# A Strassen-type up projection in the MLP of a one-core encoder layer

## Chip, cores and metric

One Trainium2 chip, one of its cores. The metric is the device time of one execution in microseconds. The engines in the profile are PE (TensorE, matmuls), PEld (TensorE's weight loads), DVE (VectorE), ACT (ScalarE), POOL (GpSimd) and SP (SyncE, which issues most DMAs).

## The reference

2176 tokens (2048 of a prompt, 128 of eight running streams) of width 1024 pass one layer:

```
h = rmsnorm(x, ln_mix); z = h @ w_in                       # 1024 x 1280
a = chunk-causal attention(q, k, v of z); b = pooling mixer(u of z)
x = x + concat(rmsnorm(a), rmsnorm(b)) @ w_out             # 1024 x 1024
x = x + square(relu(rmsnorm(x, ln_ffn) @ w_up)) @ w_down   # 1024 x 4096, 4096 x 1024
x = x + sigmoid(rmsnorm(x, ln_ple) @ w_ple_gate) * (p @ w_ple_proj)
y = rmsnorm(x, ln_final)
```

## The kernel before

Activations lie transposed: 128 features on the partitions, tokens along the free axis. The tokens form six blocks, `BLOCKS` = 256, 384, 384, 384, 384, 384. Matrix products are made in three matmuls (`mm3`, lines 117 to 119): each operand is split into a rounded high part and a low part, and high x high, low x high and high x low are summed in PSUM. The split of a weight is in `load_w`: a DMA of 512 KB, a ScalarE cast (L107) and a subtraction (L110) that falls to VectorE and GpSimd in turn, for the gates to GpSimd alone. `split` (L125, L126) and `gain_split` (L190, L191) do the same for activations. `SumSq` (L143, L144) sums squares for a norm; `rstd` and `rstd_dve` make the reciprocal root of it.

The first part, ordered by the string `SEQ_A`, is norm, input projection, attention, pooling and output projection, block by block; `out_proj` writes the new residual to the DRAM tiles `x1d`. The second part takes the blocks in pairs, `SUPER` = (1,2), (3,4), (5,0); a pair is called a super-block here. `mlp_start` loads the two blocks from `x1d` and normalises them (`load_norm`). `mlp` walks over 16 chunks of `FCH` = 2 feature tiles of 128. Per feature tile and block, up is 8 input tiles x 3 = 24 matmuls into one PSUM bank, then the squared ReLU with its split (L662, L666 to L668). Down takes, per block and output tile d, 2 x 3 matmuls and adds the bank to `acc` in SBUF (L682). After the last chunk the third norm is prepared, `gate` runs the gate and the side projection (30 matmuls per output tile), and `finish` writes out. PSUM is used as a ring of seven banks. The order of instructions on each engine is set when the program is built, by a list scheduler; on the chip each engine keeps its order and waits on semaphores.

Of the kernel before, what the change touches and what calls it, by code (L numbers as in the profile page):

```python
# [16 lines left out]
P = 128  # L17
# [9 lines left out]
SEQ_A = "I0 P1 M0 A0 K0 S0 I1 P2 M1 K1 I2 R0 A1 O0 P3 R1 M2 K2 I3 A2 O1 R2 M3 P4 K3 O2 A3 P5 R3 I4 M4 O3 A4 K4 I5 R4 M5 K5 A5 O4 R5"  # L27
SEQ_B = "X1 O5 X2"
# [4 lines left out]
QLENG = lambda nc: nc.vector  # L33
NPR = [128] + BLOCKS[1:]
# [9 lines left out]
FCH = 2  # L44
# [12 lines left out]
def hymba_step(ctx: ExitStack, tc: tile.TileContext, ins, outs):  # L57
# [10 lines left out]
    xhl = ctx.enter_context(tc.tile_pool(name="xhl", bufs=3))  # L68
# [8 lines left out]
    mask = const.tile([P, 256], F32, name="mask")  # L77
    ident = const.tile([P, P], F32, name="ident")
    invc = const.tile([P, NG, 16], F32, name="invc")
# [4 lines left out]

    x1d = [dram.tile([P, KT, n], F32, name=f"x1d{b}") for b, n in enumerate(BLOCKS)]
# [6 lines left out]
    RING = ("mm", "sc", "tr", "mm", "sc", "tr", "pv")  # L92
    ring = [0]

    def ps_ring(nm):
        ring[0] += 1
        return ps_tile(RING[ring[0] % len(RING)], nm)

    cnt = [0]

    def load_w(src, ktiles, width=P, raw_bufs=2, hl_bufs=3, tag="w", pool=None, eng=None):
        pool = pool or wp
        raw = pool.tile([P, ktiles, width], F32, tag=tag + "r", name="wraw", bufs=raw_bufs)
        nc.sync.dma_start(out=raw, in_=src)
        hi = pool.tile([P, ktiles, width], F32R, tag=tag + "h", name="whi", bufs=hl_bufs)
        lo = pool.tile([P, ktiles, width], F32R, tag=tag + "l", name="wlo", bufs=hl_bufs)
        nc.scalar.copy(out=hi, in_=raw)  # L107
        cnt[0] += 1
        eng = eng or (nc.vector if cnt[0] % 2 else nc.gpsimd)
        eng.tensor_tensor(out=lo, in0=raw, in1=hi.bitcast(F32), op=ALU.subtract)  # L110
        return hi, lo

    def mm3(ps, whl, xs, first=True, last=True):
        n = len(xs)
        hi, lo = whl
        for i, (wsel, (xh, xl)) in enumerate(xs):
            nc.tensor.matmul(ps, lhsT=wsel(hi), rhs=xh, start=first and i == 0, stop=False)  # L117
            nc.tensor.matmul(ps, lhsT=wsel(lo), rhs=xh, start=False, stop=False)  # L118
            nc.tensor.matmul(ps, lhsT=wsel(hi), rhs=xl, start=False, stop=last and i == n - 1)  # L119

    def ks(xt, N, kk):
        return [((lambda t, k=k: t[:, k, :]), (xt[0][:, k, :N], xt[1][:, k, :N])) for k in kk]
# [73 lines left out]
    def load_norm(b, src, g, hl, rstd):  # L196
        N = BLOCKS[b]
        sq = SumSq(N)
        for k in range(KT):
            x = row_tile("x")[:, :N]  # L200
            nc.sync.dma_start(out=x, in_=src[:, k, :])
            gain_split(x, g + k, hl[0][:, k, :N], hl[1][:, k, :N], LOENG[k % len(LOENG)](nc))
# [3 lines left out]
    def hl_tile(nm, pool=xhl):  # L206
        h = pool.tile([P, KT, NMAX], F32R, tag="xh", name=nm + "h")
        l = pool.tile([P, KT, NMAX], F32R, tag="xl", name=nm + "l")
        return h, l
# [9 lines left out]
    def out_proj(b):  # L219
# [4 lines left out]
        rb, ra = st_b["rb"], st_b["ra"]  # L224
        for d in range(KT):
# [13 lines left out]
            nc.sync.dma_start(out=x1d[b][:, d, :], in_=xr)  # L239

    xs, rs1 = {}, {}

    def mlp_start(b, rstd):
        xs[b] = hl_tile("x1")
        rs1[b] = load_norm(b, x1d[b], C_GFFN, xs[b], rstd)

    with tc.tile_pool(name="pa", bufs=2) as pa:
        pgain = pa.tile([P, NG], F32, name="pgain", bufs=1)
# [26 lines left out]
        def pool_mix(b, L):  # L275
            st_b = state[b]
            mh, ml = st_b["mx"]
            for g, w in enumerate(POOL_W):
# [13 lines left out]
                mhk, mlk = mh[:, 4 + g, :L], ml[:, 4 + g, :L]  # L292
# [19 lines left out]
        def pool_mix4(b, src, S, L, col):  # L312
# [33 lines left out]
            for g in range(NG):  # L346
                mm3(ps[:, g, :], (wpool_h, wpool_l), [((lambda t, g=g: t[:, g, :]), (dh[:, g, :], dl[:, g, :]))])
# [536 lines left out]
```

## Time and profile before

| | |
|---|---|
| median of 3 runs (2560.92 to 2566.02) | 2564.93 us |
| span of the profiled execution | 2563.4 us |
| PE / PEld busy | 2438.7 / 2361.4 us |
| DVE / ACT / POOL busy | 1814.0 / 874.2 / 827.8 us |
| HBM read and written | 228.44 and 18.36 MB |

The profiled execution's span, from its first instruction to its last, lies 1.5 us under the median and within the three runs. Matmuls are pipelined: the duration of one (about 0.33 us at 384 columns) overlaps the next, so the busy time of PE says that it was occupied, and the distance between starts says how fast it went.

### The profile page before, as it was taken

The page shows a single profiled execution, that of the slowest core. Times are in us where ns is not written, and L with a number is a line of the kernel's source. Part 1 is how long each engine was busy: PE and PEld are TensorE (multiplying, and loading weights), DVE is VectorE, ACT ScalarE, POOL GpSimd, SP SyncE. Part 2 cuts the span into 40 slices and gives each one's busy share as a digit, 9 for nine tenths or more (in the row PEclk, how much of TensorE's full clock was granted, in tenths as well). Part 3 has the DMA queues.
Part 4 walks back from the last instruction along what each step waited for, and adds up shares of the span by engine and source line. Part 5 has one row for each costly group of instructions (what it writes and reads, how often), then busy time and mean ns, then how long its engine had stood idle before and what let it go on. Part 6 is the DMA issues. An engine that isn't in the chain of part 4 may idle for free.

```text
span 2563.4 us, 36604 instructions
## 1 busy us (share of the span) xinstructions
PE 2438.7 (95%) x14324; PEld 2361.4 (92%) x14324; DVE 1814.0 (71%) x3113; ACT 874.2 (34%) x1601; POOL 827.8 (32%) x548
## 2 busy tenths in 40 slices
PE   7889998999899999999998999999999899999986
PEld 7888888998799999999888999999988899999986
DVE  6769888888765555555889555555587966666687
ACT  5446655445421111111652111111165212221254
POOL 4634557454631111111381111111138211111134
PEclk8989999999999999999999999999999999999998
DMA  5424335433732222222244222221234422222223
GB/s 157 129 87 137 95 120 165 138 106 97 249 102 65 59 66 66 63 62 66 91 151 158 66 66 59 66 63 59 61 102 135 136 75 75 83 74 67 83 76 113
DMA packets 104892, 249.17 MB, mean 97 GB/s; under 512 B 19600, under 2 KB 55440, under 8 KB 104720
## 3 DMA queue, kind: packets, MB, share of 16 engines
q1 hardware_dynamic: 104176, 246.32, 31.4%
q8 instruction: 112, 1.84, 0.3%
q10 hardware_dynamic: 544, 0.52, 0.1%
q14 instruction: 60, 0.49, 0.1%
HBM read 228.44 MB, written 18.36 MB: 96 GB/s over the span
## 4 chain that ended last, share of the span: by engine, by line
PE 59%; DVE 10%; ACT 2%; DMA 2%; issue 1%; POOL 0%; SPq 0%; DVEq 0%; ACTq 0%; POOLq 0%
PE ps_dn L117 10%; PE ps_dn L118 10%; PE ps_dn L119 10%; PE ps_up L119 9%; PE ps_up L118 9%; PE ps_up L117 9%; DVE sqa L144 2%; DVE acc L714 1%; DVE x1l L191 1%; DVE x2l L191 1%; DMA x<-x1d 1%; DVE rs_t L159 1%; DMA xr<-in_xT 1%; ACT whi L107 1%; DVE acc L737 1%
## 5 line engine op out<-in xcount | busy, mean ns | idle before, releaser
L110 POOL TENSOR_TENSOR wlo<-wraw,whi 128x1024 fp32r<-128x1024 f32 (+1 forms) x245 | 533.0, 2182 | 1466.9 <-ACT whi L107 1452.1
L107 ACT CAST whi<-wraw 128x1024 fp32r<-128x1024 f32 (+1 forms) x395 | 377.1, 968 | 999.8 <-issue 578.5
L682 DVE TENSOR_TENSOR acc<-ps_dn,acc 128x384 f32<-128x384 f32 (+1 forms) x768 | 389.6, 530 | 167.9 <-PE ps_dn L119 166.9
L117 PE MATMUL ps_dn<-hh,whi 128*128 128x384 f32 (+1 forms) x1536 | 500.0, 327 | 4.5 <-DVE r L662 4.5
L119 PE MATMUL ps_up<-x1l,whi 128*128 128x384 f32 (+1 forms) x1536 | 501.0, 326 | 1.2 <-DVE x1l L191 1.2
L117 PE MATMUL ps_up<-x1h,whi 128*128 128x384 f32 (+1 forms) x1536 | 501.4, 327 | 0.7 <-ACT x1h L190 0.7
L118 PE MATMUL ps_up<-x1h,wlo 128*128 128x384 f32 (+1 forms) x1536 | 501.9, 327 | 0.0
L118 PE MATMUL ps_dn<-hh,wlo 128*128 128x384 f32 (+1 forms) x1536 | 499.4, 327 | 0.0
L119 PE MATMUL ps_dn<-hl,whi 128*128 128x384 f32 (+1 forms) x1536 | 488.0, 326 | 0.0
L117 PEld LDWEIGHTS ps_dn<-hh,whi 128*128 128x128 f32 x1536 | 290.8, 189 | 5.1 <-DVE r L662 5.1
L119 PEld LDWEIGHTS ps_up<-x1l,whi 128*128 128x128 f32 x1536 | 290.2, 189 | 2.0 <-DVE x1l L191 1.5
L117 PEld LDWEIGHTS ps_up<-x1h,whi 128*128 128x128 f32 x1536 | 290.1, 189 | 1.3 <-ACT x1h L190 1.0
L118 PEld LDWEIGHTS ps_up<-x1h,wlo 128*128 128x128 f32 x1536 | 290.3, 189 | 0.7 <-issue 0.6
L118 PEld LDWEIGHTS ps_dn<-hh,wlo 128*128 128x128 f32 x1536 | 290.8, 189 | 0.0
L119 PEld LDWEIGHTS ps_dn<-hl,whi 128*128 128x128 f32 x1536 | 289.0, 189 | 0.2 <-DVE hl L668 0.2
L662 DVE SCALAR_TENSOR_TENSOR r<-ps_up,sqa 128x384 f32<-128x384 f32 x192 | 102.1, 535 | 254.2 <-PE ps_up L119 254.0
L667 DVE TENSOR_TENSOR r<-r 128x384 f32<-128x384 f32 x192 | 191.2, 998 | 97.4 <-ACT hh L666 97.4
L110 DVE TENSOR_TENSOR wlo<-wraw,whi 128x1024 fp32r<-128x1024 f32 x150 | 191.0, 1273 | 56.4 <-ACT whi L107 54.1
L666 ACT ACTIVATE hh<-r 128x384 fp32r<-128x384 f32 x192 | 96.3, 504 | 300.2 <-DVE r L662 300.0
L117 PE MATMUL ps_in<-xnh,whi 128*128 128x384 f32 (+1 forms) x472 | 162.9, 345 | 12.9 <-DVE z L561 5.5
L118 PE MATMUL ps_in<-xnh,wlo 128*128 128x384 f32 (+1 forms) x472 | 161.2, 342 | 2.7 <-POOL wlo L110 2.0
L119 PE MATMUL ps_in<-xnl,whi 128*128 128x384 f32 (+1 forms) x472 | 159.6, 339 | 0.0
(208 smaller groups left out, 3992.4 us busy)
## 6 DMA issues: line engine op xcount, KB each, us to landing
wraw<-in_w_up SPq DMA_DIRECT2D x96, 512.0 KB, 3.7
wraw<-in_w_down SPq DMA_DIRECT2D x96, 512.0 KB, 3.6
wraw<-in_w_in SPq DMA_DIRECT2D x59, 512.0 KB, 3.7
wraw<-in_w_out SPq DMA_DIRECT2D x48, 512.0 KB, 3.7
wraw<-in_w_gate SPq DMA_DIRECT2D x48, 512.0 KB, 3.6
x<-in_xT SPq DMA_DIRECT2D x40, 192.0 KB, 2.6
xr<-in_xT SPq DMA_DIRECT2D x40, 192.0 KB, 3.2
x1d<-xr SPq DMA_DIRECT2D x40, 192.0 KB, 2.1
```

The source lines that it names most:

```text
L107: nc.scalar.copy(out=hi, in_=raw)
L110: eng.tensor_tensor(out=lo, in0=raw, in1=hi.bitcast(F32), op=ALU.subtract)
L117: nc.tensor.matmul(ps, lhsT=wsel(hi), rhs=xh, start=first and i == 0, stop=False)
L118: nc.tensor.matmul(ps, lhsT=wsel(lo), rhs=xh, start=False, stop=False)
L119: nc.tensor.matmul(ps, lhsT=wsel(hi), rhs=xl, start=False, stop=last and i == n - 1)
L144: eng.tensor_tensor(out=o, in0=o, in1=t, op=ALU.add)
L159: V.tensor_tensor(out=u, in0=u, in1=y, op=ALU.mult)
L191: eng.scalar_tensor_tensor(out=lo, in0=src, scalar=c, in1=hi.bitcast(F32), op0=ALU.mult, op1=ALU.subtract)
L662: nc.vector.scalar_tensor_tensor(out=r, in0=ps, scalar=0.0, in1=rs1[b], op0=ALU.max, op1=ALU.mult)
L666: nc.scalar.activation(out=hh, in_=r, func=AF.Square)
L667: nc.vector.tensor_tensor(out=r, in0=r, in1=r, op=ALU.mult)
L682: nc.vector.tensor_tensor(out=acc[b][:, d, :N], in0=ps, in1=acc[b][:, d, :N], op=ALU.add)
```

## The change

Up is done on 2x2 blocks: two feature tiles (output halves), two halves of 512 inputs (4 input tiles each), two halves of the tokens of a super-block. Seven products replace eight, in Strassen's manner with shared sums. With A the weight blocks and B the normalised activations:

```
S1 = A21+A22   S2 = S1-A11   S3 = A11-A21   S4 = A12-S2
T1 = B12-B11   T2 = B22-T1   T3 = B22-B12   T4 = B21-T2
products: A11*B11, S2*T2, A12*B21, S1*T1, S3*T3, S4*B22, A22*T4
```

The weight sums are made on GpSimd in every pass over a feature pair; sums and blocks are then split into high and low parts. The activation operands (7 with high and low part, 4 input tiles each) are made once per super-block, in `comb`, from rows of `x1d` and the roots stored in `rsd`, with four subtractions on GpSimd per step; the four steps are put between output tiles of the block-5 output projection, or of the last down chunk of the super-block before (`fill`). The block products are added on VectorE into rows in SBUF, and the squared ReLU reads SBUF.

The tokens of the second part are cut into six halves of 364, 364, 364, 364, 360, 360 (`CUTS`), so that the two halves of a super-block are equal. Down goes in chunks of `FCH` = 4 feature tiles: 12 matmuls per output tile, half and chunk, 8 chunks; its weight tensor is laid out anew, and a piece of 4 tiles (256 KB) serves both halves, but is loaded for each half in the last chunk. All weights come in such units of 4 tiles, with 6 raw buffers and 5 each for high and low parts. Sums of squares for the MLP norm move from `load_norm` into `out_proj`, the root into `out_fin`, called at the places `F0` to `F4` of `SEQ_A`. The order in the second part: two or three feature pairs of up lead, then each down chunk is followed by two more; the second gate of a super-block (`tail`) stands between feature pairs of the next one. The PSUM ring is divided: up uses the four banks `sc` and `tr`, down and gates the three of `mm` and `pv`.

```diff
-SUPER = [(1, 2), (3, 4), (5, 0)]
+CUTS = [256, 620, 984, 1348, 1712, 2072, 2432]
-FCH = 2
+FCH = 4
+NWR, NWL, NWH = 6, 5, 5
+    def load_u(src, eng=None):
+        raw = wp.tile([P, 4, P], F32, tag="wr", name="wraw", bufs=NWR)
         nc.sync.dma_start(out=raw, in_=src)
         cnt[0] += 1
+        return split_u(raw, eng or (nc.vector if cnt[0] % 2 else nc.gpsimd))
...
     def out_proj(b, fill=()):
+        sq = st_b["sq1"] = SumSq(N)
...
+            sq.add(xr, eng=nc.gpsimd)
+            if d % 2 and fill:
+                fill.pop(0)()
+    def out_fin(b):
+        rs = state[b]["sq1"].rstd(D, ps_tile("ms", "ps_ms"))
+        nc.sync.dma_start(out=rsd[b], in_=rs)
...
+        def comb(s, rs, k):
+            for kk in range(2):
+                for i in range(2):
+                    x = r[kk, i] = row("xr", "xc", n)
+                    for b, c, o in pieces(2 * s + i):
+                        nc.sync.dma_start(out=x[:, o], in_=x1d[b][:, kt, c])
+                    nc.vector.scalar_tensor_tensor(out=x, in0=x, scalar=gain, in1=rs[i], op0=ALU.mult, op1=ALU.mult)
+            put("B11", b11)
+            sub(b11, b12, b11)
+            put("T1", b11)
...
+        def up(s, p):
+            for nm, f, k0 in (("A11", 2 * p, 0), ("A21", 2 * p + 1, 0), ("A22", 2 * p + 1, 4), ("A12", 2 * p, 4)):
+                raw[nm] = raw_u(nm)
+                nc.sync.dma_start(out=raw[nm], in_=w_up[f][:, k0 : k0 + 4, :])
+            wsum("S1", "A21", "A22", ALU.add)
+            wsum("S2", "S1", "A11", ALU.subtract)
+            wt = {"A11": split_u(raw["A11"], nc.vector), "S2": split_u(raw["S2"], nc.vector)}
+            wsum("S3", "A11", "A21", ALU.subtract)
+            wsum("S4", "A12", "S2", ALU.subtract)
+            for nm, eng in zip(WOPS[2:], (nc.gpsimd, nc.vector, nc.vector, nc.vector, nc.gpsimd)):
+                wt[nm] = split_u(raw[nm], eng)
+            def prod(w, o):
+                ps = ps_tile(("sc", "tr")[up_ring[0] % 2], "ps_up")[:, :n]
+                mm3(ps, WU([wt[w]]), [(k, (xh[:, k, :n], xl[:, k, :n])) for k in range(4)])
+            def hidden(x, i):
+                nc.vector.scalar_tensor_tensor(out=x, in0=x, scalar=0.0, in1=x, op0=ALU.max, op1=ALU.mult)
+                split(x, hh[:, i, :n], hl[:, i, :n], nc.vector)
+            nc.scalar.copy(out=x11, in_=prod("A11", "B11"))
+            add(u, prod("S2", "T2"), x11)
+            add(x11, prod("A12", "B21"), x11)
+            hidden(x11, 0)
+            add(v, prod("S1", "T1"), u)
+            p7 = prod("S3", "T3")
+            add(u, p7, u)
+            add(x22, p7, v)
+            hidden(x22, 3)
+            add(v, prod("S4", "B22"), v)
+            hidden(v, 1)
+            add(u, prod("A22", "T4"), u)
+            hidden(u, 2)
...
+        for s in range(3):
+            if s == 0:
+                up(s, 0)
+                up(s, 1)
+            else:
+                up(s, 0)
+                finish(2 * s - 2)
+                tail(s - 1, 2 * s - 1)
+                up(s, 1)
+                finish(2 * s - 1)
+            up(s, 2)
+            acc_load(s)
+            for c in range(NPAIR // 2 - 1):
+                down(s, c)
+                up(s, 2 * c + 3)
+                if 2 * c + 4 < NPAIR:
+                    up(s, 2 * c + 4)
+            fill = [] if last else comb_steps(s + 1)
+            down_last(s, fill)
+            for f in fill:
+                f()
+            tail(s, 2 * s)
```

## Rows read from the trace of the kernel before

**Rows 1.** Page: span, and the first row of the busy times

```profile
span 2563.4 us, 36604 instructions
...
PE 2438.7 (95%) x14324; PEld 2361.4 (92%) x14324; DVE 1814.0 (71%) x3113; ACT 874.2 (34%) x1601; POOL 827.8 (32%) x548
```

**Rows 2.** Windows of the span: busy us of each engine (instructions), clock, DMA

```profile
core 0: us, PE busy (x) PEld busy (x) DVE busy (x) ACT busy (x) POOL busy (x), PEclk, DMA share, GB/s
0.00:200.00 200.00, 170.00 (x932) 156.74 (x933) 143.38 (x287) 94.24 (x203) 100.89 (x96) 0.89 0.45 125
200.00:640.00 440.00, 425.84 (x2427) 382.87 (x2427) 386.00 (x836) 242.59 (x561) 230.77 (x189) 0.99 0.40 123
640.00:720.00 80.00, 66.30 (x341) 61.17 (x340) 60.23 (x77) 35.60 (x61) 52.92 (x40) 0.94 0.70 242
720.00:1240.00 520.00, 520.00 (x2999) 519.51 (x2998) 310.06 (x486) 104.00 (x146) 80.03 (x34) 1.00 0.22 66
1240.00:1380.00 140.00, 119.31 (x641) 113.52 (x640) 125.52 (x171) 76.15 (x133) 82.29 (x49) 0.96 0.42 133
1380.00:1880.00 500.00, 500.00 (x2887) 500.00 (x2886) 299.98 (x470) 93.10 (x126) 75.57 (x31) 1.00 0.24 72
1880.00:2020.00 140.00, 121.93 (x662) 116.14 (x661) 120.69 (x178) 79.51 (x143) 78.61 (x49) 0.95 0.40 124
2020.00:2440.00 420.00, 420.00 (x2859) 420.00 (x2858) 271.78 (x470) 86.33 (x121) 72.33 (x30) 1.00 0.26 79
2440.00:2563.00 123.00, 95.32 (x592) 91.43 (x590) 96.32 (x146) 62.67 (x115) 54.43 (x32) 0.89 0.31 94
```

**Rows 3.** Timeline of PE inside the third super-block: start, duration

```profile
2209.82 0.33 PE L118 MATMUL ps_up<-x1h,wlo 128*128 128x384 f32 x1
...
2212.77 0.28 PE L117 MATMUL ps_up<-x1h,whi 128*128 128x256 f32 x1
...
2215.64 0.34 PE L117 MATMUL ps_dn<-hh,whi 128*128 128x384 f32 x1
```

**Rows 4.** Source lines: count, duration in ns min/median/max, first and last start

```profile
L682 DVE TENSOR_TENSOR acc<-ps_dn,acc x768: 411/548/558, 733.3 to 2462.3; 128x384 f32<-128x384 f32 x160, 128x256 f32<-128x256 f32 x32
...
L667 DVE TENSOR_TENSOR r<-r x192: 416/559/2440, 719.1 to 2442.4; 128x384 f32<-128x384 f32 x160, 128x256 f32<-128x256 f32 x32
...
L110 DVE TENSOR_TENSOR wlo<-wraw,whi x150: 1208/1226/2158, 17.1 to 2435.1; 128x1024 fp32r<-128x1024 f32 x150
...
L126 POOL TENSOR_TENSOR mxl<-ag,mxh x19: 1282/1302/2297, 80.0 to 664.1; 128x512 fp32r<-128x512 f32 x19
```

**Rows 5.** Timeline of POOL and DVE in the first super-block

```profile
1027.72 2.40 POOL L110 TENSOR_TENSOR wlo<-wraw,whi 128x1024 fp32r<-128x1024 f32 x1 [13.73 <-ACT whi L107]
...
1028.10 2.44 DVE L667 TENSOR_TENSOR r<-r 128x384 f32<-128x384 f32 x1 [0.99 <-ACT hh L666]
```

**Rows 6.** Groups of POOL by form: busy us, mean ns | idle before

```profile
L110 POOL TENSOR_TENSOR wlo<-wraw,whi 128x1024 fp32r<-128x1024 f32 x197 | 483.6, 2456 | 1440.6 <-ACT whi L107 1425.7 <-DVE sbuf L479 8.3 <-DMA wraw<-in_w_out 3.8
L144 POOL TENSOR_TENSOR sqa<-sqa,sqt 128x384 f32<-128x384 f32 x70 | 86.9, 1241 | 29.5 <-ACT sqt L143 26.9 <-ACT st L408 0.6 <-ACT sqa L139 0.5
L110 POOL TENSOR_TENSOR wlo<-wraw,whi 128x256 fp32r<-128x256 f32 x48 | 50.7, 1057 | 26.4 <-ACT whi L107 26.4
...
L286 POOL TENSOR_TENSOR pt<-ext 128x386 f32<-128x386 f32 x5 | 4.2, 832 | 8.1 <-DVE ext L589 7.4 <-DVE st L405 0.7
```

**Rows 7.** Page: one of its costliest groups, the squaring

```profile
L667 DVE TENSOR_TENSOR r<-r 128x384 f32<-128x384 f32 x192 | 191.2, 998 | 97.4 <-ACT hh L666 97.4
```

**Rows 8.** Page: DMA issues, KB each, median us to landing

```profile
x<-x1d SPq DMA_DIRECT2D x40, 192.0 KB, 3.3
```

**Rows 9.** Timeline of PE after a gap of 6.43 us

```profile
1365.64 0.52 PE L119 MATMUL ps_up<-x1l,whi 128*128 128x384 f32 x1
1365.96 0.52 PE L117 MATMUL ps_up<-x1h,whi 128*128 128x384 f32 x1
...
1367.82 0.33 PE L117 MATMUL ps_up<-x1h,whi 128*128 128x384 f32 x1
```

More of the change, by code (lines that the diff above doesn't have):

```diff
@@ L83, in hymba_step, with half @@
     nc.vector.memset(eps_t, EPS)
+    def half(t, k, h):
+        o = HSTART[h] * k * P
+        return t[o : o + P * k * HN[h]].rearrange("(p k n) -> p k n", p=P, k=k)
+    rsd = [dram.tile([P, n], F32, name=f"rsd{b}") for b, n in enumerate(BLOCKS)]
     x1d = [dram.tile([P, KT, n], F32, name=f"x1d{b}") for b, n in enumerate(BLOCKS)]
@@ L111, in load_w @@
         return hi, lo
+    def load_w(src, ktiles):
+        return WU([load_u(src[:, k : k + 4, :]) for k in range(0, ktiles, 4)])
     def mm3(ps, whl, xs, first=True, last=True):
         n = len(xs)
[L115 to L119, printed above, removed]
+        for i, (wk, (xh, xl)) in enumerate(xs):
+            nc.tensor.matmul(ps, lhsT=whl.hi(wk), rhs=xh, start=first and i == 0, stop=False)
+            nc.tensor.matmul(ps, lhsT=whl.lo(wk), rhs=xh, start=False, stop=False)
+            nc.tensor.matmul(ps, lhsT=whl.hi(wk), rhs=xl, start=False, stop=last and i == n - 1)
@@ new lines, in drop, with row, pieces, comb_begin @@
+        def drop(*ts):
+            for t in ts:
+                free[pool_of.pop(id(t))[0]] += 1
+        def row(tag, nm, n, dt=F32):
+            return tmp.tile([P, NMAX], dt, tag=tag, name=nm, bufs=ROWS[tag])[:, :n]
+        def pieces(h):
+            o = 0
+            for b, c0, c1 in HALVES[h]:
+                yield b, slice(c0, c1), slice(o, o + c1 - c0)
+                o += c1 - c0
+        ops, acc, hq, x2, sqs = {}, {}, {}, {}, {}
+        up_ring = [0]
+        free[Q1] -= 4
+        def comb_begin(s):
+            ops[s] = {o: (take(o + "h"), take(o + "l")) for o in OPS}
+            n = HN[2 * s]
+            rs = [row("sqa", "rs1", n) for _ in range(2)]
+            for i in range(2):
+                for b, c, o in pieces(2 * s + i):
+                    nc.sync.dma_start(out=rs[i][:, o], in_=rsd[b][:, c])
+            return rs
@@ new lines, in acc_load, with down @@
+        def acc_load(s):
+            for h in (2 * s, 2 * s + 1):
+                acc[h] = [take("acc", Q1) for _ in range(2)]
+                for i in range(2):
+                    for b, c, o in pieces(h):
+                        nc.sync.dma_start(
+                            out=acc[h][i][:, :, o].bitcast(F32), in_=x1d[b][:, 4 * i : 4 * i + 4, c]
+                        )
+        def down(s, c):
+            for d in range(KT):
+                wu = WU([down_unit(c, d)])
+                for h in (2 * s, 2 * s + 1):
+                    down_one(s, c, d, h, wu)
+            drop(*hq[s, 2 * c], *hq[s, 2 * c + 1])
@@ new lines, in finish @@
+            drop(*acc[h])
+        st = comb_steps(0)
+        out_proj(5, st)
+        for f in st:
+            f()
+        out_fin(5)
+        free[Q1] += 4
+        for s in range(3):
+            last = s == 2
+            if s == 0:
+                up(s, 0)
+                up(s, 1)
+            else:
+                up(s, 0)
[13 more added lines that the diff above has]
+            for f in fill:
+                f()
+            tail(s, 2 * s)
+            if last:
+                finish(2 * s)
+                tail(s, 2 * s + 1)
+                finish(2 * s + 1)
```

383 lines of the change are left out of this document (211 added, 172 removed).

## The prediction, made before the change was run

> **What bounds the kernel now.** I read the page's busy shares first. TensorE is busy 95% of the span and VectorE 71% [rows 1]. A share is an average over stages, so next I cut the span into its stages [rows 2]. In the stretch 720 to 1240 TensorE is busy for all 520.00 us; 1380 to 1880 looks the same, and so does 2020 to 2440. There nothing but matmuls sets the time. The time that TensorE loses lies elsewhere: 30 us up to 200, 14 us from 200 to 640, 14 at the seam 640 to 720, 21 and 18 at the two seams between super-blocks, 28 at the end.
>
> Third view: the timeline of TensorE, for the price of one matmul [rows 3]. Durations of matmuls overlap, so the distance between starts counts. From 2209.82 to 2212.77 lie 17 matmuls of 384 columns: 173.5 ns each. The 24 of 256 columns from 2212.77 to 2215.64 take 119.6 each. A column thus costs 0.421 ns and an instruction 11.8 ns whatever its width; the count in the windows agrees, 520 us / 2999 = 173.4. So 364 columns cost 165.1 ns and 360 cost 163.4.
>
> Fourth: what VectorE and GpSimd do to each other. VectorE's 384-column operations take 0.55 to 0.56 us at the median [rows 4], but the squaring L667 goes up to 2.44. In the timeline it starts while GpSimd's 2.40 us weight subtraction runs and ends with it [rows 5]: an operation with both inputs in SBUF stands still beside GpSimd. The one that reads PSUM, L682, never exceeds 0.558 [rows 4].
>
> **The change: matmuls.** Before, up and down each take 24 matmuls per feature tile (or output tile and its share) and block: 1536 per block pair and projection, both projections 3072 per pair. Pairs one and two: 2 x 3072 x 173.5 ns = 1066.0 us. The third pair is 384 and 256 wide: 1536 x (173.5 + 119.6) = 450.2. Together 1516.2 us.
> After, up needs 7 products x 4 input tiles x 3 matmuls = 84 per feature pair, 16 pairs, 1344 per super-block instead of 1536; down stays at 1536. So 2880 x (165.1 + 165.1 + 163.4) ns = 1421.6 us. The gates keep 240 matmuls per block, 236.9 us before and after. **Matmul term: -94.6 us.** It counts in full because those stretches have no idle time to absorb it.
> [...]
>
> **The change: what replaces them, per feature pair.** VectorE, at 0.535 us for 364 columns (0.559 less 20 columns at (0.559 - 0.416)/128) and 0.69 for a 512-wide subtraction (between 0.559 and 1.226, rows 4): 7 additions out of PSUM 3.7 us, 4 x 2 operations for the squared ReLU and its low part 4.3, 5 low parts of weights 3.4; total 11.4. GpSimd: 4 weight sums and 2 low parts. The 512-wide subtraction takes 1.30 us [rows 4]; the plain 386-wide sum 0.83 [rows 6], so 1.1 for 512. Total 7.0 us. TensorE needs 84 x 165.1 = 13.9 us.
> So each engine alone fits. But 7.7 us of VectorE's work has two SBUF inputs and excludes GpSimd's 7.0: 14.7 us, more than 13.9; and if every GpSimd operation stops VectorE for its whole length, 11.4 + 7.0 = 18.4. The down chunk that follows every two pairs is the relief: TensorE 8 x 24 x 165.1 ns = 31.7 us, VectorE 16 x 0.535 + 4 x 0.69 = 11.3, GpSimd 4 x 1.3 = 5.2. Over the cycle of two ups and one down TensorE has 59.5 us, VectorE at the very worst 2 x 18.4 + 16.5 = 53.3. On average it fits; what counts is whether the lag of two ups can be carried. Four PSUM banks hold up's products, so VectorE may lag three products, 3 x 12 x 0.165 = 5.9 us, before TensorE waits.
> Bounds: if GpSimd stops nothing, no lag; if it stops VectorE always, 2 x (18.4 - 13.9) = 9.0 us, of which 3.1 stall, 24 cycles, 74 us. Today VectorE loses in L667 191.2 - 160 x 0.559 - 32 x 0.416 = 88 us [rows 7], of the 228 us that GpSimd works in the three saturated stretches [rows 2]: 39%. VectorE is fuller after the change (34 of 59.5 us before blocking, and in the ups 11.4 of 13.9), so I take 60%: a lag of 2 x (11.4 + 4.2 - 13.9) = 3.4 us, inside 5.9. Before each squaring VectorE waits for ScalarE today, 97.4 us in 192 times, 0.51 each [rows 7]; if nothing is put in between, four such waits per pair raise the lag to 7.5 us, 1.6 of it stall. **Term: +10 us**, 0.4 per cycle, because unlike now there is other VectorE work to put there; ends 0 and 74.
> Fewer accumulations (384 instead of 768 of L682) and the chunk of four remove VectorE work from stretches in which it has room; they earn nothing by themselves and are what makes the room above. ScalarE is busy 104 of 520 us there [rows 2] and gets one PSUM copy per pair more and an eighth less of weight casts: no cost. Weight loads are twice as many and half as large, at 22% of DMA time [rows 2], with six buffers ahead: no cost either; without that cover a load of about 3.3 us [rows 8] would stand bare once per unit.
>
> **Front part (to 640).** Each output projection now also squares and sums its result, and `out_fin` makes the reciprocal root. For blocks 0 to 4 that is 35 GpSimd additions at 1.24 us [rows 6], 43 us, in a stretch where VectorE is busy 386 of 440 us and TensorE idles 14 [rows 2]. Weights come in two halves: two weights cost 2 x (0.69 + 1.30) = 4.0 us instead of 1.23 + 2.46, some 15 us over 100 weights. With 40 to 60% of 43 us stopping VectorE, 17 to 26 us fall on its 54 us of room. **+12 us**; ends 0 and 26.
>
> **Seam at 640 to 720.** Operands of the first super-block: 4 steps x 11 operations x 0.535 = 23.5 us of VectorE and 16 x 0.8 = 12.8 of GpSimd, all excluding each other, 36 us; before, two normalised loads: 16 x 0.56 + 14 x 1.24 = 26. The output projection of block 5 gains 7 sums, 9 us. So +19 us at a place where TensorE already idles, and its first product waits for all four steps. Each step reloads its rows into four buffers (3.3 us to land [rows 8]), behind the step before. The loads are queued on SP among weight loads. Operand tiles lie in the memory that attention frees, so they can't start before it ends. **+15**; ends 0 (hidden under attention's end) and 35.
>
> **Seams at 1240 and 1880.** The same 36 us of operand work replaces 26 plus two roots of eleven VectorE operations (12 us): about equal. The last down chunk loads its weights per half: 16 units averaging 1.0 us instead of 7.3 for four tiles, +8; 14 squares summed on GpSimd instead of VectorE, +5; gate weights in 20 halves of 1.30 instead of 8 x 2.46 + 8 x 1.06 [rows 6], -2 for each gate. About +10 us per seam on two engines that are together at 208 busy of 140 [rows 2]. TensorE gets up products between the two gates to fill in, but these use the same two engines. The operand steps stand between the additions of the last chunk in VectorE's queue; where a step waits for its load or for a GpSimd subtraction, the additions behind it wait too, and TensorE after three banks, 3 x 12 x 0.165 = 5.9 us. **+20 for both**; ends 0 and 50.
>
> **End.** The last block has 360 columns, not 256: the root chain and the closing multiplications, some 12 operations, are each 104 x 0.0011 us longer, and the last store moves more bytes. **+2**, ends 0 and 5.
>
> Sum: -94.6 + 10 + 12 + 15 + 20 + 2 = -35.6. The profiled span is 2563.4 and the median of runs 2564.9, 1.5 more; 2563.4 - 35.6 + 1.5 = **2529 us**. For this kernel under 0.2%, 5 us, is no measurable change.
>
> **Rivals.**
> Full gain (0.22): seams and front part hide all of it; ups between the gates give TensorE work where it idles 39 us now. For it: the front part has 54 us of free VectorE time, and the seams now have nothing but gates to run. Against it: VectorE and GpSimd leave no room in the seams. 2564.9 - 94.6 + 2 = 2472.
> The lock decides, slower (0.14): in every cycle VectorE falls behind beyond the four banks. Place: the ups; price 3.1 us x 24 = 74 instead of 10, 2529 + 64 = 2593. It turns the sign from 1.9 us of stall per cycle, (35.6 + 10)/24. After a gap TensorE also runs at half pace: 0.32 us per matmul from 1365.64 to about 1367.6, against 0.17 later [rows 9], so a stall costs more than its length. For it: 14.7 against 13.9. Against: L682 never slowed, and the down chunk gives 31.7 us in which VectorE needs 11 to 17.
> [...]
> The seams eat it (0.14): front part, first seam and the two others at their upper ends, 26 + 35 + 50, ups clean: 2564.9 - 94.6 + 111 + 2 = 2583; with the first seam at 15 instead of 35, about 2563. For it: operand steps in series, each behind a load and a GpSimd subtraction. Against: gate matmuls, 40 us each, stand beside them.
>
> **How the numbers follow.** Forecast, 2505 to 2555: 0.50. The cases give faster 0.76 (forecast, full gain, a third of the seams case), same 0.06, slower 0.18. Range 2472 to 2585: holds the forecast, half of the full-gain case and the seams case.
>
> **What would show it.** Right: 1344 up matmuls per super-block at 0.165 us pitch; the stretch of a whole cycle near 60 us; VectorE 75 to 90% busy in it; means of two-SBUF operations well above 0.54 and PSUM additions at it. Wrong: TensorE waiting on VectorE's additions in every pair of ups, or a granted clock below 1.00 there, means the lock; seams no longer than before mean the full gain; new idle time of 40 us or more per seam with TensorE waiting for operands means that the seams eat it.

## The result, and the profile after

The changed kernel takes 2627.82 us (median of 4 runs, 2623.65 to 2632.23), the kernel before 2564.31 on the same chip: ratio 1.0251, 95% interval 1.0235 to 1.0267. It is 63.5 us slower; the forecast was 36 us faster.

The page of the kernel after, its span and first row of busy times, to be read beside [rows 1]:

```profile
span 2623.6 us, 38643 instructions
...
PE 2377.0 (91%) x13748; PEld 2288.6 (87%) x13748; DVE 1776.2 (68%) x3188; ACT 1078.0 (41%) x2192; POOL 1236.9 (47%) x1022
```

TensorE has 576 matmuls less and is busy 62 us less, in a span that is 60 us longer. VectorE did not become fuller over the whole; GpSimd did, by 409 us. The windows by stage say where the time lies, beside [rows 2]; columns are the same:

```profile
core 0: us, PE busy (x) PEld busy (x) DVE busy (x) ACT busy (x) POOL busy (x), PEclk, DMA share, GB/s
0.00:650.00 650.00, 593.78 (x3356) 541.30 (x3357) 523.27 (x1185) 368.16 (x904) 371.24 (x361) 0.95 0.42 122
650.00:790.00 140.00, 103.95 (x483) 93.75 (x482) 110.38 (x153) 54.54 (x106) 91.25 (x75) 0.84 0.40 120
790.00:1210.00 420.00, 420.00 (x2528) 420.00 (x2527) 239.98 (x418) 125.05 (x222) 144.12 (x109) 1.00 0.26 80
1210.00:1440.00 230.00, 171.70 (x971) 164.52 (x970) 177.16 (x254) 106.91 (x199) 135.37 (x101) 0.89 0.41 123
1440.00:1830.00 390.00, 390.00 (x2348) 390.00 (x2348) 222.09 (x386) 115.45 (x206) 137.42 (x104) 1.00 0.23 70
1830.00:2090.00 260.00, 203.08 (x1132) 192.93 (x1131) 192.83 (x280) 115.23 (x212) 145.26 (x110) 0.89 0.38 114
2090.00:2430.00 340.00, 340.00 (x2074) 340.00 (x2073) 200.54 (x351) 105.16 (x188) 122.98 (x93) 1.00 0.23 73
2430.00:2624.00 194.00, 154.50 (x870) 146.08 (x868) 109.92 (x166) 87.48 (x157) 89.24 (x71) 0.92 0.30 94
```

Two things are to be seen. The stretches of up and down are saturated: TensorE busy 100%, clock 1.00, 2528 matmuls in 420 us. And the seams are long and hollow. Busy time hides how hollow, so I count matmuls. Inside the saturated stretches 100 us hold 604 of 364 columns, 0.1656 us each, and up to 613 of 360, 0.163:

```profile
800.00:900.00 100.00, 100.00 (x604) 100.00 (x603) 53.04 (x93) 26.89 (x48) 36.86 (x29) 1.00 0.27 85
2100.00:2200.00 100.00, 100.00 (x613) 100.00 (x612) 61.54 (x108) 31.68 (x57) 34.63 (x26) 1.00 0.25 79
```

A window less its count times that price is the time lost in it:

| stretch | lost before [rows 2, 3] | lost after | more | forecast |
|---|---|---|---|---|
| to 650 (matmuls priced by width) | | | 9 | 12 |
| ups and downs: 0.1661 us per matmul against 0.1651 forecast, 0.1639 against 0.1634 | | | 6 | 10 |
| first seam (341 x 0.1735; by width) | 21 | 58 | 37 | 15 |
| second: 140 - 641 x 0.1735; 230 - 971 x 0.1656 | 29 | 69 | 40 | 10 |
| third: 140 - 662 x 0.1735; 260 - 1132 x 0.1656 | 25 | 72 | 47 | 10 |
| end (by width); 194 - 870 x 0.163 | 37 | 52 | 15 | 2 |
| sum | | | 154 | 59 |

94.6 us of matmuls saved and 154 lost make 59; the two spans differ by 60. So the account closes to a few us, and the question is what fills the seams with waiting. TensorE's waits over the whole span name one first; in the kernel before, the longest entry of this list is 13.0 us, and none is for rows of p:

```profile
engine line waited for: us in total, times, longest us
PE ps_ple L148 <- ACT pth L159: 92.1, 7, 33.4
...
PE ps_ob L148 <- DVE ot L269: 11.4, 6, 5.3
PE ps_dn L148 <- DVE acc L825: 10.9, 12, 2.8
```

`pth` is the high part of the gate's second operand, two rows of p per half that the function `tail` loads. TensorE's timeline at the first gate of super-block 0:

```profile
1243.94 0.33 PE L150 MATMUL ps_dn<-hl,whi 128*128 128x364 f32 x1
1277.70 0.67 PE L148 MATMUL ps_ple<-pth,whi 128*128 128x364 f32 x1 [33.43 <-ACT pth L159]
1278.17 0.51 PE L149 MATMUL ps_ple<-pth,wlo 128*128 128x364 f32 x1
1278.48 0.51 PE L148 MATMUL ps_gt<-x2h,whi 128*128 128x364 f32 x1
...
1281.72 0.32 PE L150 MATMUL ps_gt<-x2l,whi 128*128 128x364 f32 x1
```

ScalarE's timeline in that gap shows what stands ahead of the cast of `pth`:

```profile
1271.01 0.49 ACT L159 CAST B11h<-xc 128x364 fp32r<-128x364 f32 x1 [2.21 <-DVE xc L718]
1273.96 0.49 ACT L159 CAST B21h<-xc 128x364 fp32r<-128x364 f32 x1 [2.45 <-DVE xc L718]
...
1277.15 0.49 ACT L159 CAST pth<-ptr 128x364 fp32r<-128x364 f32 x1 [0.80 <-DVE T3l L160]
```

It was released by `T3l`, made from a row of the last operand step. The high and low rows of p are taken from the ring `xr` of four row buffers, and `comb` takes all four for each of its steps. So the gate cannot start before the last step has given a buffer back. The first of the four steps is nearly done before TensorE stops; the rest of the second runs while it stands, and so do the third (casts from 1260.27) and the fourth (from 1271.01), bare and one behind the other. It is the same from 1882 to 1909, a wait of 27.42 us.

The second gate has another gap. TensorE's, SyncE's and VectorE's timelines beside it:

```profile
1355.22 0.67 PE L148 MATMUL ps_ple<-pth,whi 128*128 128x364 f32 x1 [9.54 <-ACT pth L159]
```

```profile
1352.32 0.33 SPq L870 DMA_DIRECT2D ptr<-in_pT  x1
...
1356.31 0.35 SPq L870 DMA_DIRECT2D ptr<-in_pT  x1
```

```profile
1347.18 0.54 DVE L192 SCALAR_TENSOR_TENSOR rs_t<-sqa,rs_t 128x364 f32<-128x364 f32 x1
...
1351.75 0.54 DVE L194 SCALAR_TENSOR_TENSOR sqa<-rs_t 128x364 f32<-128x364 f32 x1
1352.32 4.86 DVE L909 SCALAR_TENSOR_TENSOR acc<-acc,cv_sb,sqa 128x364 f32<-128x364 f32 x8
```

The raw row `ptr` comes from the ring `rt` of two, which holds the root's scratch rows `rs_t` of `finish`. Its load is issued at 1352.32, when the last operation of the root that reads them is done; TensorE stands from 1345.7 to 1355.22.

### The profile page after: what moved, and what is told of

It is laid out like the page before. It is cut to its first block, busy times and chain, and to the rows that moved or that the text cites. A ratio compares the mean times of both kernels' runs of the same rounds, so it can differ in the third digit from the quotient of the medians.

```text
span 2623.6 us, 38643 instructions
## 1 busy us (share of the span) xinstructions
PE 2377.0 (91%) x13748; PEld 2288.6 (87%) x13748; DVE 1776.2 (68%) x3188; ACT 1078.0 (41%) x2192; POOL 1236.9 (47%) x1022
## 4 chain that ended last, share of the span: by engine, by line
PE 61%; DVE 11%; DMA 3%; POOL 3%; issue 3%; ACT 2%; SPq 0%; DVEq 0%; POOLq 0%; ACTq 0%
PE ps_dn L148 9%; PE ps_dn L149 9%; PE ps_dn L150 9%; PE ps_up L148 8%; PE ps_up L150 8%; PE ps_up L149 8%; POOL wlo L160 2%; PE ps_gt L148 2%; DVE wlo L160 2%; PE ps_gt L149 1%; PE ps_gt L150 1%; DVE x2l L225 1%; DMA xc<-x1d 1%; PE ps_in L148 1%; PE ps_in L150 1%
## 5 line engine op out<-in xcount | busy, mean ns | idle before, releaser
L160 POOL TENSOR_TENSOR wlo<-wraw,whi 128x512 fp32r<-128x512 f32 x335 | 462.0, 1382 | 391.2 <-ACT whi L159 332.1
L159 ACT CAST whi<-wraw 128x512 fp32r<-128x512 f32 x552 | 339.2, 618 | 508.2 <-PE ps_dn L150 155.8
L148 PE MATMUL ps_dn<-hh,whi 128*128 128x364 f32 (+1 forms) x1536 | 507.1, 330 | 13.1 <-DVE acc L825 10.9
L149 PE MATMUL ps_dn<-hh,wlo 128*128 128x364 f32 (+1 forms) x1536 | 505.8, 329 | 0.0
L150 PE MATMUL ps_dn<-hl,whi 128*128 128x364 f32 (+1 forms) x1536 | 505.4, 330 | 0.0
L825 DVE TENSOR_TENSOR acc<-ps_dn,acc 128x364 f32<-128x364 f32 (+1 forms) x384 | 203.5, 533 | 356.1 <-PE ps_dn L150 355.9
L160 DVE TENSOR_TENSOR wlo<-wraw,whi 128x512 fp32r<-128x512 f32 x217 | 182.4, 841 | 22.0 <-ACT whi L159 19.5
L178 POOL TENSOR_TENSOR sqa<-sqa,sqt 128x384 f32<-128x384 f32 (+3 forms) x119 | 136.0, 1144 | 48.0 <-ACT sqt L177 45.5
L148 PE MATMUL ps_gt<-x2h,whi 128*128 128x364 f32 (+1 forms) x384 | 131.1, 342 | 15.7 <-ACT whi L159 5.8
L149 PE MATMUL ps_gt<-x2h,wlo 128*128 128x364 f32 (+1 forms) x384 | 128.3, 334 | 0.0
```

The source lines that it names most:

```text
L148: nc.tensor.matmul(ps, lhsT=whl.hi(wk), rhs=xh, start=first and i == 0, stop=False)
L149: nc.tensor.matmul(ps, lhsT=whl.lo(wk), rhs=xh, start=False, stop=False)
L150: nc.tensor.matmul(ps, lhsT=whl.hi(wk), rhs=xl, start=False, stop=last and i == n - 1)
L159: nc.scalar.copy(out=hi, in_=src)
L160: lo_eng.tensor_tensor(out=lo, in0=src, in1=hi.bitcast(F32), op=ALU.subtract)
L178: eng.tensor_tensor(out=o, in0=o, in1=t, op=ALU.add)
```

## The experiments

Times stand beside a run of the kernel before on the same chip, 2561.72 to 2563.14 us. Every version is scheduled anew when it is built, so what an edit brings includes what the new order of the other instructions brings; no run kept that order. The first theory was R: rows of p wait for buffers of other work. Its rival L: VectorE and GpSimd have too much to do in the seams, and the gate only shows it.

**Own rows for p, and a control.** One tile of the operand pool is given up for the room; the control gives it up and does nothing else.

```diff
-NQ1, NQ2 = 12, 13
+NQ1, NQ2 = 12, 12
-                l, hi, r = row("xr", "ptl", n, F32R), row("xr", "pth", n, F32R), row("rt", "ptr", n)
+                l = pb.tile([P, HMAX], F32R, tag="ptl", name="ptl", bufs=2)[:, :n]
+                hi, r = pb.tile([P, HMAX], F32R, tag="pth", name="pth", bufs=2)[:, :n], row("rt", "ptr", n)
```

> The high and low rows of the side input get four rows of their own in the second part's memory instead of the ring `xr` (one operand quad less pays for them); the raw row stays in `rt`. Theory R (rows): the first gate of a super-block stands still because its side-input rows queue behind the operand steps' rows, so the gaps of about 35 and 31 us at the two inner seams close: 45 to 70 us faster than the changed kernel, 2558 to 2583. Theory L (load): VectorE and GpSimd together have too much to do there; the gate starts earlier, the next up starts as late as before: at most 15 us faster, 2613 or more.

> Control for the run with own rows: only the operand quad less (12 instead of 13 in the second part). Both theories: within 8 us of the changed kernel, 2620 to 2636. If it is 20 us or more slower, the supply of quads itself is a bound in the seams and the own-rows run is read against this one.

Measured: 2602.06 us (ratio 1.0152, 1.0134 to 1.0169), 26 less than the changed kernel, between the ranges of R and L; the control 2629.44 (1.0255, 1.0236 to 1.0274), no change. The waits for `pth` fell from 92.1 to 33.3 us, but the two inner seams still lose 230 - 1034 x 0.1656 = 59 and 260 - 1242 x 0.1656 = 54 us. The shared ring is a cause, and not all of it.

**No operand steps in the inner seams.**

```diff
-            fill = [] if last else comb_steps(s + 1)
+            fill = []
+            if not last:
+                ops[s + 1] = ops[s]
```

> Leaves out the operand steps of the second and third super-blocks: their up products reuse the first one's operands, so the MLP of tokens 728 on is computed from other tokens' operands. Shows what these steps cost at the two inner seams in all. Theory R and L alike: 70 to 110 us faster than the changed kernel, 2518 to 2558. Under R the own-rows run gets at least half of this, under L hardly any.

Measured: 2570.46 (1.0033, 1.0023 to 1.0044), 57 us less, below the 70 to 110 of both theories. If the 26 of the ring are part of it, the steps themselves cost some 31; and even without them the kernel is slower than before. TensorE still waits 45.1 us for p rows, in 8 waits of 9.7 at most: some 23 at the two inner second gates, whose raw rows stand behind the root, 15 at the two inner first gates and 7 at the end.

**The second gate ahead of `finish`.**

```diff
-                finish(2 * s - 2)
                 tail(s - 1, 2 * s - 1)
+                finish(2 * s - 2)
                 up(s, 1)
```

> Order only: the second gate of a super-block is written before the finish of its first half, also at the end. Theory R: the second gate waits for a row of `rt` that the finish's root holds (gaps of 10 to 17 us, then half clock); 20 to 35 us faster, 2593 to 2608. Theory L: the same work in another order, at most 8 us.

Measured: 2623.06 (1.0230, 1.0213 to 1.0248), 5 us less, as L said; the intervals of this and of the changed kernel overlap. The waits of this run show why the order alone brought so little:

```profile
PE ps_ple L148 <- ACT pth L159: 51.7, 5, 19.1
PE ps_ms L208 <- POOL sqa L178: 21.0, 4, 12.1
```

`pth` waits fell, and the root waited for sums of squares queued on GpSimd instead.

**Three guesses at crowding, on top of the own rows.** Steps spread over the last down chunk and the gate; the low parts of the gate's weights taken by VectorE and GpSimd in turn; both, with the second gate ahead of `finish`. And one step in place of four in the first seam of the changed kernel.

```diff
-                    if d % 2 and fill:
+                    if d == 3 and fill:
                         fill.pop(0)()
...
+                if d in (1, 4) and fill:
+                    fill.pop(0)()
```

```diff
-                    wpl = WU([load_u(w_ple[d // 2], eng=nc.gpsimd)])
-                whl = WU([load_u(w_gate[d][:, 4 * i : 4 * i + 4, :], eng=nc.gpsimd) for i in range(2)])
+                    wpl = WU([load_u(w_ple[d // 2])])
+                whl = WU([load_u(w_gate[d][:, 4 * i : 4 * i + 4, :]) for i in range(2)])
```

```diff
         def comb(s, rs, k):
+            if s == 0 and k:
+                return
...
-[(k, (xh[:, k, :n], xl[:, k, :n])) for k in range(4)])
+[(k, (xh[:, k * (s > 0), :n], xl[:, k * (s > 0), :n])) for k in range(4)])
```

> On top of the gate's own rows (2602.06 us in its run), the four operand steps of super-blocks 1 and 2 are spread: one in each half of the last down chunk and two in the first gate, instead of four in the first half of the chunk. Theory C (crowding: four steps bring VectorE and GpSimd more work than the some 16 us of matmuls they stand beside, and the matmuls wait for it): most of what the steps still cost, 2602 minus 2570 = 32 us for both seams, comes back: 2570 to 2588 us. Rival R (chain: what costs is the way of the last step's rows through DMA, VectorE and GpSimd into the next super-block's first product, wherever the steps stand): later steps end later, so no gain or a loss: 2598 to 2620 us.

> On top of the gate's own rows: the low parts of the gate's weights alternate between VectorE and GpSimd instead of standing on GpSimd alone. If GpSimd's 1.29 us for each low part sets the pace of the gates (55 to 56 matmuls per 10 us in place of 60 to 61, six gates of some 40 us): 18 us less, 2580 to 2592 us. If the pace is set by the chain through the gate's own output rows and sums: 2597 to 2607 us, or more, as VectorE gets more to do.

> Own rows, spread steps, alternating low parts and the second gate ahead of the finish of the first half, together. If the theories of the single runs hold (32 of the steps less 10, 15 of the gates, 5 to 20 of the second gate): 2530 to 2560 us, faster than the kernel before. If the seams lose by chains that only move: 2580 to 2605 us.

> The changed kernel, in the first super-block with one operand step instead of four; its products read the first quarter of each operand in place of the other three. It leaves out three quarters of the normalized input of super-block 0. Theory C: the first seam's extra loss, some 35 to 50 us over the kernel before, is from the steps, which stand beside an output projection that needs the same engines: 2585 to 2600 us. Rival P (the loss is from the output projection's own longer start and the weight sums of the first up): 2615 to 2628 us.

Measured: spread 2605.32 (1.0169, 1.0154 to 1.0184), gate weights 2601.24 (1.0148, 1.0128 to 1.0168), all three 2593.2 (1.0120, 1.0103 to 1.0137). Against 2602.06 with the own rows alone the first two are nothing, the three together 9 us. The theory of crowding as I had put it falls: spreading the steps in this way does not matter. First seam: 2606.51 (1.0176, 1.0159 to 1.0193), 21 us less for three steps, between the ranges of the two theories; in proportion, an estimate, all four cost some 28 of the 37 that this seam lost more.

**Early p rows.** Own rows alone left `ptr` in the ring of the root. Now it stands in the ring of the gate's output rows, and the 24 gate products go ahead of the 6 p products.

```diff
-                hi, r = pb.tile([P, HMAX], F32R, tag="pth", name="pth", bufs=2)[:, :n], row("rt", "ptr", n)
+                hi, r = pb.tile([P, HMAX], F32R, tag="pth", name="pth", bufs=2)[:, :n], row("ot", "ptr", n)
...
-                pe = ps_dn("ps_ple")[:, :n]
-                mm3(pe, wpl, [(2 * (d % 2) + k, pt[k]) for k in range(2)])
                 ps = ps_dn("ps_gt")[:, :n]
                 mm3(ps, whl, xs)
+                pe = ps_dn("ps_ple")[:, :n]
+                mm3(pe, wpl, [(2 * (d % 2) + k, pt[k]) for k in range(2)])
```

> On top of the gate's own rows (2602.06 us in its run): the raw row of the gate's p operand no longer stands in the ring of the root's scratch row, where its second load waits for the root of the sums; it stands in the ring of the gate's output rows, and each gate output takes its 24 gate products ahead of its 6 p products. Theory W (waits for p rows that came late, 12 to 15 us of TensorE's waiting at each inner seam and more by the half-paced clock behind each gap): 20 to 40 us less, 2562 to 2582 us. Rival V (VectorE's work is what is late there, and the p rows are only the first to show it): the wait moves to the gate's own output rows, 2594 to 2604 us.

> The same, with the second gate ahead of the finish of the first half (its root of 11 and its 8 multiplications on VectorE, some 13 us, stand ahead of the second gate in the changed kernel). Alone this gave 5 us. If the finish is what stops the second gate once the p rows are early: 15 to 25 us under the run with early p rows alone. If it only moves ahead of the next up: within 6 us of it.

> The same again, with the operand steps spread over the last down chunk and the first gate. On the gate's own rows alone the spread changed nothing (2605 to 2602 us). Theory W: with no wait for p rows in its way it now gives 10 to 20 us, which brings the time to 2530 to 2560 us. Rival V (an operand step takes VectorE some 12 us wherever it stands, because GpSimd works beside it: 1.1 to 1.2 us for an operation that takes 0.54 alone): within 6 us of the run without the spread.

Measured: 2571.39 (1.0031, 1.0020 to 1.0043), 31 us less, in the range of theory W. The edit makes two changes at once, the ring and the order of the products, and no run tells them apart. The wait for p rows is gone from the list; its longest entry is now one for the gate's output rows, as the rival V had it, at a time that V had not:

```profile
PE ps_ple L148 <- DVE sg L886: 47.5, 9, 13.8
```

With the second gate ahead of `finish` 2562.95 (0.9999, 0.9990 to 1.0009): 8 us, more than the 5 alone and less than the 15 hoped for. The spread on top, 2563.57 (1.0000, 0.9991 to 1.0010), again nothing. At this point the change costs and saves the same. What TensorE waits for in the second seam (1200 to 1420) of the version with early p rows and the second gate first:

```profile
PE ps_ple L148 <- DVE sg L886: 12.2, 6, 6.2
PE ps_up L149 <- DVE wlo L160: 6.4, 2, 4.4
PE ps_gt L148 <- DVE sg L888: 3.6, 3, 2.3
```

Now it is VectorE in each of these waits, 196.25 us busy of 220 in that seam. A few microseconds of it and of GpSimd:

```profile
1227.76 0.97 DVE L825 TENSOR_TENSOR acc<-ps_dn,acc 128x364 f32<-128x364 f32 x2
...
1229.45 1.30 DVE L160 TENSOR_TENSOR T1l<-xc,T1h 128x364 fp32r<-128x364 f32 x1
1230.68 0.97 DVE L825 TENSOR_TENSOR acc<-ps_dn,acc 128x364 f32<-128x364 f32 x2
...
1238.39 1.18 DVE L718 SCALAR_TENSOR_TENSOR xc<-xc,cv_sb,rs 128x364 f32<-128x364 f32 x1
```

```profile
1228.95 1.42 POOL L178 TENSOR_TENSOR sqa<-sqa,sqt 128x364 f32<-128x364 f32 x1
1230.33 1.27 POOL L728 TENSOR_TENSOR xc<-xc 128x364 f32<-128x364 f32 x1
...
1237.58 1.59 POOL L160 TENSOR_TENSOR wlo<-wraw,whi 128x512 fp32r<-128x512 f32 x1
1239.14 1.27 POOL L728 TENSOR_TENSOR xc<-xc 128x364 f32<-128x364 f32 x1
```

The additions out of PSUM take 0.97 for two; the operations with both inputs in SBUF take 1.18 to 1.30 instead of some 0.54 to 0.59, and both shown end 0.4 us after an operation of GpSimd that had begun before them (1230.75 against 1230.37, 1239.57 against 1239.17). They took 1.30 us beside 1.42 and 1.18 beside 1.59; by what means the one would hold up the other no run shows. That GpSimd's results simply come late is a rival that the traces do not bear out: among the seven longest waits of TensorE in that stretch, and the seven of VectorE in the second seam of the changed kernel (1210 to 1440), none ends with an operation of GpSimd. So two theories were left. V: GpSimd's operations hold VectorE up in the seams. N: the amount of VectorE's own work is too large there.

**Work moved from GpSimd to VectorE.** The four subtractions of each step, on the version of 2562.95 us and alone in the changed kernel; then also the sums of squares of the last down chunk; then also the sums of the last output projection (with the spread), or the gate's weights.

```diff
             def sub(x, a, b):
-                nc.gpsimd.tensor_tensor(out=x, in0=a, in1=b, op=ALU.subtract)
+                nc.vector.tensor_tensor(out=x, in0=a, in1=b, op=ALU.subtract)
...
-                    sq.add(a, eng=nc.gpsimd)
+                    sq.add(a, eng=nc.vector)
...
-                whl = WU([load_u(w_gate[d][:, 4 * i : 4 * i + 4, :], eng=nc.gpsimd) for i in range(2)])
+                whl = WU([load_u(w_gate[d][:, 4 * i : 4 * i + 4, :]) for i in range(2)])
...
-                    wpl = WU([load_u(w_ple[d // 2], eng=nc.gpsimd)])
+                    wpl = WU([load_u(w_ple[d // 2], eng=nc.vector)])
...
-            sq.add(xr, eng=nc.gpsimd)
+            sq.add(xr, eng=nc.vector if fill else nc.gpsimd)
```

> Early p rows and the second gate ahead of the finish, with the operand steps' four subtractions on VectorE instead of GpSimd. Theory V (VectorE is held up by GpSimd: each of the 16 subtractions of a seam takes GpSimd 1.15 us, in which VectorE's operations from SBUF stand still): VectorE loses 16 x 0.54 us and gains up to 16 x 1.15: 5 to 15 us less in all over three seams. If only the count of VectorE's operations matters: 10 to 25 us more.

Measured: 2552.18 (0.9956, 0.9942 to 0.9970), 11 us less, with more work on VectorE: theory V.

> The changed kernel with nothing but the operand steps' four subtractions on VectorE. With the late p rows still in the way I expect less than the 10.8 us that it gave without them: 2612 to 2626 us against 2627.82 us by theory V; 2628 to 2645 us by theory N.

Measured: 2623.46 (1.0245, 1.0228 to 1.0262), 4 us less. The intervals of this and of the changed kernel overlap, so it speaks for V weakly; it suggests that with the late p rows in the way most of the 11 us are not to be had.

> The same version without the spread, with the sums of squares of the last down chunk on VectorE (0.54 us each alone) instead of GpSimd (1.24 us): 14 operations for each of three seams. Theory V: 3 to 12 us less. Theory N: VectorE gets 7.6 us more work in each seam, 10 to 20 us more.

Measured: 2543.68 (0.9936, 0.9919 to 0.9953), 8 us less, in V's range. The interval overlaps a little with that of the run with only the subtractions moved on this version (0.9942 to 0.9970), so alone this is weak; the run with the sums of the first seam moved too, below, has the same edit and stays as low.

> The version with early p rows, the second gate ahead of the finish and the subtractions on VectorE (2552.18 us in its run), with the operand steps spread over the last down chunk and the first gate. Theory N (VectorE's amount of work in a seam is what is left: 17 to 20 of every 20 us there): spreading it over a longer stretch gives 5 to 15 us. Theory V (GpSimd beside VectorE): within 5 us, as in the run before it.

Measured: 2551.45 (0.9956, 0.9939 to 0.9973): the spread is nothing for the third time.

> The version with early p rows, the second gate ahead of the finish and the subtractions on VectorE, but the operands of super-block 0 are read again in 1 and 2: it leaves out the 8 operand steps of the inner seams and so computes the up projection of the wrong tokens there. Theory N: the steps are most of what the inner seams lose beyond the 29 and 30 us of the kernel before, and more, as VectorE gets 33 us of each seam back: 2500 to 2525 us. Theory V: with the subtractions moved, the steps cost little more: 2530 to 2545 us.

Measured: 2521.49 (0.9844, 0.9825 to 0.9863), 31 us less than with the steps, in the range of N. The windows of its two inner seams:

```profile
1200.00:1400.00 200.00, 181.64 (x1015) 177.44 (x1014) 152.46 (x223) 96.52 (x177) 115.35 (x85) 0.94 0.42 128
1780.00:2020.00 240.00, 223.00 (x1284) 218.82 (x1283) 171.90 (x259) 109.32 (x199) 132.73 (x99) 0.96 0.39 119
```

They lose 200 - 1015 x 0.1656 = 32 and 240 - 1284 x 0.1656 = 27 us, about what the kernel before lost, which had two normalised loads there. With the steps it is 45 and 44: each seam's four steps still cost some 15 us. V and N both hold: GpSimd beside VectorE costs part, the steps themselves another. Whether by VectorE's work or by their loads and casts, this run does not tell.

> The version with the sums of the last down chunk on VectorE (2543.68 us in its run), with the sums of the last output projection on VectorE too, and the inner operand steps spread. Theory V: another 8 GpSimd operations of 1.24 us gone beside a crowded VectorE, 3 to 8 us less, 2535 to 2541 us. Theory N: VectorE has 18 of 20 us of work in the first seam and gets 4 us more: 2543 to 2550 us.

> The version with the sums of the last down chunk on VectorE, with the low parts of the gate's weights taken in turn by VectorE and GpSimd and those of the p weights on VectorE. Theory V: VectorE gives 0.69 us for each low part and is freed of 1.3 us of GpSimd, 60 low parts: 5 to 20 us less. Theory N: the gates' VectorE work grows by 7 us each and shows in the time: 2550 to 2575 us.

Measured: 2545.69 (0.9932, 0.9916 to 0.9949) with the sums of the first seam moved, no gain, in the range of N. With the gate's weights 2520.53 (0.9842, 0.9825 to 0.9858), 23 us less than without, a little more than V's range. On top of the own rows alone much the same edit had brought 1 us. This version beats the kernel before by 1.6%. Its windows:

```profile
1180.00:1400.00 220.00, 197.62 (x1118) 191.28 (x1117) 202.03 (x335) 114.14 (x216) 75.79 (x51) 0.96 0.44 138
...
1780.00:2020.00 240.00, 218.65 (x1249) 211.82 (x1248) 209.37 (x350) 118.27 (x225) 92.16 (x61) 0.97 0.42 129
...
2360.00:2513.00 153.00, 135.85 (x808) 132.20 (x806) 118.28 (x196) 84.17 (x154) 41.96 (x32) 0.97 0.37 116
```

The inner seams lose 35 and 33 us, the end 153 - 808 x 0.163 = 21, under the 37 of the kernel before. VectorE is busy 92% of the second seam, GpSimd 34% (59% of it in the changed kernel). This profiled execution took 2514.67 us, 6 under the median of its kernel, so of these losses 1 or 2 us each may be missing.

What V says of VectorE can be read in the traces themselves. The four operations that open each step, 48 in all, in the version of 2562.95 us and in the last one (nanoseconds: least, median, most); the median is 596 already with the subtractions moved:

```profile
L718 DVE SCALAR_TENSOR_TENSOR xc<-xc,cv_sb,rs x48: 580/1070/1645, 690.3 to 1912.3; 128x364 f32<-128x364 f32 x32, 128x360 f32<-128x360 f32 x16
```

```profile
L718 DVE SCALAR_TENSOR_TENSOR xc<-xc,cv_sb,rs x48: 580/592/1627, 686.2 to 1878.1; 128x364 f32<-128x364 f32 x32, 128x360 f32<-128x360 f32 x16
```

For the whole second seam an estimate can be made: the time of every VectorE operation with both inputs in SBUF, less what it takes alone (0.53 us, 0.69 for 512 columns). That is some 66 us of standing still in the version of 2562.95 us, about half of GpSimd's 139 us there, 59 with the subtractions moved, 59 with the sums moved, 37 in the last version, where VectorE does the most work.

## Why the prediction was wrong

**Matmul term, -94.6: right.** 0.1656 us per matmul against 165.1 ns forecast, in stretches that stayed full.

**VectorE beside GpSimd in the ups, +10: 6, near by luck.** That VectorE's 7.7 us from SBUF and GpSimd's 7.0 exclude each other was my estimate from one pair of operations, 2.44 us beside 2.40 [rows 5]. "I take 60%", the share of GpSimd's time that stops VectorE, was wrong here: by the same estimate as for the seam, from 800 to 1200 VectorE stands still for some 14 us beside GpSimd's 138, a tenth. VectorE is busy 56% of that stretch, where the sign of being right was 75 to 90%, and TensorE has no wait in it; the 6 us are a pace of 0.1661 us per matmul in place of 0.1651, half of which is in the price itself. The rival "The lock decides", its name for VectorE standing still beside GpSimd, is refuted there: TensorE is busy 100.00 of 100 us at clock 1.00 in the ups.

**Front part, +12: 9.** The size was right; no run took apart what it is made of.

**Seam at 640 to 720, +15: too small, 37.** The step was there ("its first product waits for all four steps") and the price was not: three of four steps alone are 21 us. I took a step as work that fills room; TensorE waited in this seam for the evictions of the output projection (`ps_ob`, 11.0 us behind `ot`, 6.3 before) and then for the operands (`B11h`, 6.1 us).

**Seams at 1240 and 1880, +20 for both: the step that failed.** It measured some 87. "The same 36 us of operand work replaces 26 plus two roots: about equal" compared amounts, and the sentence against the rival, "gate matmuls, 40 us each, stand beside them", took it that the gate could run beside the steps. It could not: the gate's own p rows were behind the steps and the roots in the rings `xr` and `rt`. The kernel before gave p buffers outside these rings (`praw`, `pp`, a tile of the hidden rows); the change took them away, and neither my list of what is removed nor that of added waits had it. By the experiments, in the order in which they were taken away: the shared ring `xr` 26 us, the ring `rt` with the order of the products 31, `finish` ahead of the second gate 8, and the three pieces of work on GpSimd 11, 8 and 23, 107 together; these numbers hold for that order only and span the end of the kernel too.

**End, +2: too small, 15.** The last gate has the same late rows; with early p rows the end (2400 to 2570) loses 170 - 838 x 0.163 = 33 us, less than before.

**The rival "The seams eat it" was the right one**, and its mark, new idle time of 40 us or more per seam with TensorE waiting for operands, was met in part: 40 and 47 us more were lost in the inner seams and 37 in the first, and in the inner ones TensorE waited for rows of p, not for operands. Its price of 2583 was too low, because its ends were those of the same terms. The full gain never came near: no version tried lost less in the first seam than some 52 us, but for the one that left three steps out.

**Open:** why four steps cost the same wherever in the seam they stand. That VectorE is busy some 90% of it argues for its amount of work, but no run made that work itself cheaper, and the last version gave VectorE more of it and was faster. Nor was the first seam's remainder (58 less 28 for the steps, against 21 before) taken apart.

## What to carry to other kernels

When a change moves or merges buffers, list for each row that a stage loads at its start which ring it comes from and who holds that ring then: a row that waits for the stage before turns parallel work into a series (92.1 us of waits for `pth` here), and no sum of busy times shows it. Take away the waits first and weigh engines after: an edit that relieves GpSimd brought 1 us behind the late rows and 23 once they, and some of GpSimd's other work, were out of the way. Where VectorE sets the pace, count a part of GpSimd's time as VectorE's, and read from the trace how large: here, by estimate, about half in a seam (66 us of 139) and a tenth in the ups (14 of 138). Moving work from GpSimd to the fuller engine can then make the kernel faster, here by 11, 8 and 23 us.

## What was not expected of the hardware

A seam was relieved by loading its busiest engine. The stretch 1200 to 1420 of the version of 2562.95 us, and of that with the subtractions moved:

```profile
1200.00:1420.00 220.00, 187.15 (x1028) 179.88 (x1028) 196.25 (x266) 109.09 (x207) 139.03 (x103) 0.94 0.43 131
```

```profile
1200.00:1420.00 220.00, 191.42 (x1058) 185.03 (x1057) 196.24 (x284) 107.34 (x203) 124.97 (x89) 0.95 0.43 133
```

VectorE does 284 operations in the time of 266, and TensorE gets 1058 matmuls through instead of 1028: the operations from SBUF stood still less, 59 us against 66 by the estimate above.

What a gap costs beside its length differs between two seams of the changed kernel. In the first seam after, TensorE is idle for 140 - 103.95 = 36 us, in waits of at most 6.1, and 58 are lost: 22 went to matmuls below full pace, at a mean granted clock of 0.84 over the stretch. In the second seam 58 of 69 us are idle, more than half of it in one gap, and 11 are pace; after this gap of 33.43 us, with a granted clock of 0.50 in the last 20 us of it (1258 to 1278), matmuls start 0.30 us apart from 1278.17 and 0.16 apart again from 1281.72, some 2 us for the longest gap of all.
